# Where the inverse roots of boundary norms are computed, in what order a first weight slab is loaded, and where one value product of the second memory stands

## The chip, the cores and the metric

The kernel runs on one core of a Trainium2 chip. The metric is the device time of one execution in microseconds, the median of several. The engines are named as in the profile: PE is TensorE's matmul, PEld its weight load, DVE is VectorE, ACT is ScalarE, POOL is GpSimd, and SP is SyncE, which here issues DMAs. Each engine works through its own instructions in order; engines wait for one another by semaphores.

## The reference

Two transformer blocks run one after the other on x (512 tokens by 1024), each with its own memory of 256 tokens. Everything is float32. Cut to its skeleton:

```python
def first_block(x, mem, ...):
    mem_n = rmsnorm(mem, mem_norm)
    mk, mv = memory_kv(mem_n, mem_w_kv[0], ...)
    x = mlstm_layer(x, ..., mk, mv, ...)            # A
    k_sh, v_sh = shared_kv(x, ...)                  # reads rmsnorm(x, kv_norm)
    mk, mv = memory_kv(mem_n, mem_w_kv[1], ...)
    return mla_layer(x, ..., k_sh, v_sh, ..., mk, mv, ...)   # B

def second_block(x, mem, ...):
    h = rms_norm(x, g_mix)
    x = x + mixed(h) @ w_out                        # pooling, differential attention, gates
    hc = rms_norm(x, g_cross)
    x = x + memory_cross_attention(hc, rms_norm(mem, g_mem), w_cq, w_ckv, w_co)
    x = x + jnp.square(jax.nn.relu(rms_norm(x, g_mlp) @ w_up)) @ w_down
    return rms_norm(x, g_final)

def rmsnorm(t, g):
    return t * lax.rsqrt(jnp.mean(t * t, axis=-1, keepdims=True) + EPS) * g
```

What matters here is the norm of a token block: the mean square of its 1024 elements, its inverse root, and the scaling of the block. In the cross attention the second memory's values are mem_n times a half of w_ckv, 256 x 1024.

## The kernel before

A float32 product is made of three matmuls (`mm3`): each operand is split into a high and a low half, and high x high, high x low and low x high are summed in PSUM. The high half is made by ACT as a copy (`whi`, `xth`, `mt`, `cvh`), the low half by DVE as a difference (`wlo`, `xtl`, `mt`, `cvl`). Weights come in slabs of 1 MB. SP issues a slab's DMA into one of two raw buffers (`wraw`), and then four pieces of it are split by ACT (L285) and DVE (L286) into one of two pairs `whi`, `wlo`. A raw buffer is loaded again when its four pieces are split. The program is a list of units, `prog`, which `emit` walks in order. A unit issues its matmuls and the work behind them; between units a few pieces of the next slab are split. So the order on each engine is the order of the units with the pieces in between, and it is fixed when the program is built.

x is kept as four token blocks of 128 (tb0 to tb3), each in two halves of 512 (`xs[tb][h]`, in the profile `xall`). The norm of a block has these steps:

- `norm_half`: ACT squares a half and sums it (`junk`, L582).
- `norm_rsqrt`: two instructions on DVE make the mean (`nv`, L586 and L587), one makes a first guess of the inverse root by integer arithmetic (`rsy`, L546). Then `newton` makes six dependent instructions on 128 x 1 elements (L547, L549, and L552 four times, `rsx` and `rst`). They run on POOL unless `eng` is given. In the kernel before it is given for the first memory block alone.
- `norm_scale`: DVE multiplies both halves by `rst` (`xn`, L594 without a gain, L596 with one).
- `norm_T`: PE transposes a half in four blocks (`tr`, L602), ACT and DVE split it (`xth`, `xtl`).

`boundary` orders this between two layers. `op` are the eight products of an output projection, two for each token block; each ends in an addition to `xall` on DVE (L669). For each block come the first product, the transposes of two blocks earlier, the first square, the scaling of the block before, the second product, the second square with `norm_rsqrt`, and then what `mid` gives. The scaling of tb0 stands behind the norm of tb1. Behind the blocks come the first unit of `fa`, the scaling of tb3, the second unit of `fa`, the transposes of tb2, the rest of `fa`, `fb`, and the transposes of tb3. It is used four times: from A to B (no gain, around 455 to 487 us), from B to the second block's mix (846 to 888), ahead of the cross attention (1118 to 1148) and ahead of the feed-forward part (1258 to 1287).

At the start, `load_mem(i)` issues the DMAs of a memory block's two halves, `dma_first(i)` that of the i-th slab. `stat` is the two squares and `norm_rsqrt`; `xst` and `xsc` are the norms and scalings of the four x blocks, which stand between the products of the first memory (`mk0`, in the profile `mkv`).

`cross_v(s)` makes a quarter of the second memory's values: 24 matmuls for each of two memory token blocks into one PSUM bank `cv`, then the split into `cvh` and `cvl`. Its units `cvs` stand at the end of the mix and in the cross boundary.

Of the kernel before, what the change touches and what calls it, by code (L numbers as in the profile page):

```python
# [26 lines left out]
def block_kernel(ctx: ExitStack, tc: tile.TileContext, A: dict, out: bass.AP, stop=None):  # L27
    nc = tc.nc
# [649 lines left out]
    def boundary(op, mid={}, fa=(), fb=(), gain=False):  # L678

        sts = [dict() for _ in range(4)]  # L680
        res = []

        def trans(tb):
            return [U(lambda h=h: norm_T(sts[tb], tb, h, xt_dst(S["xt"])), quiet=True) for h in range(2)]

        def scale(tb):
            return U(lambda: norm_scale(sts[tb], xs[tb], S["gain"] if gain else None), quiet=True)

        for tb in range(4):
            st = sts[tb]  # L690
            res.append(op[2 * tb][0:3] + ("last",))
            if tb > 1:
                res += trans(tb - 2)
            res += [U(lambda st=st, tb=tb: norm_half(st, xs[tb][0], 0), quiet=True)]
            if tb > 1:
                res.append(scale(tb - 1))
            res += [op[2 * tb + 1][0:3] + ("last",),
                    U(lambda st=st, tb=tb: (norm_half(st, xs[tb][1], 1), norm_rsqrt(st)), quiet=True)]
            if tb == 1:
                res.append(scale(tb - 1))  # L700
            res += mid.get(tb, [])
        fa = list(fa)
        return res + fa[0:1] + [scale(3)] + fa[1:2] + trans(2) + fa[2:] + list(fb) + trans(3)
# [227 lines left out]
    def stat(st, srcs, eng=None):  # L931
# [4 lines left out]
    stx = [dict() for _ in range(4)]  # L936
    mT = [[U(lambda i=i, h=h: norm_T(st0[i], i, h, mt_tiles)) for h in range(2)] for i in range(2)]
    xT = [[U(lambda tb=tb, h=h: norm_T(stx[tb], tb, h, xt_dst(S["xt"]))) for h in range(2)] for tb in range(4)]
    xst = [U(lambda tb=tb: stat(stx[tb], xs[tb])) for tb in range(4)]
    xsc = [U(lambda tb=tb: norm_scale(stx[tb], xs[tb], S["gain"])) for tb in range(4)]  # L940
    mk0 = mem_kv_units(0, "mt")
    add(U(lambda: load_mem(1)), U(lambda: dma_first(0)), U(lambda: S.update(gain=gain_tiles(A["a_norm"], eng=nc.sync))), U(lambda: load_x([0])),
        U(lambda: dma_first(1)), U(lambda: load_x([1, 2, 3])), U(load_constants))
    add(U(lambda: stat(st0[0], mem0[0], eng=dve)), U(lambda: norm_scale(st0[0], mem0[0], S["mgain"], inplace=True)),
        U(lambda: stat(st0[1], mem0[1])), mT[0], (None, 1, False, False), mk0[0][0], U(lambda: norm_scale(st0[1], mem0[1], S["mgain"], inplace=True)), mT[1], xst[0],
        (None, 10000, False, False))
    kd = U(lambda: some_constants(5))
    add(mk0[0][1], xsc[0], xst[1], kd, mk0[1], mk0[6], xT[0], xsc[1], xst[2], kd, mk0[2], mk0[7], xT[1], xsc[2], xst[3], kd, mk0[3], xT[2], xsc[3], kd, kd)
# [659 lines left out]
        return U(fn, cslab(("ckv", s), w_ckv, 256 * s, 256))  # L1608

    def cross_v(s):  # L1610
        def fn(w):
            ps = bank([128, 2, 256], "cv")
            for i in range(2):
                m2_product(ps[:, i, :], w, i, True)
            cv = S["cv"]
            c = slice(256 * s, 256 * s + 256)
            return lambda: split(cv[0][:, :, c], cv[1][:, :, c], ps)

        return U(fn, cslab(("ckv", 4 + s), w_ckv, 1024 + 256 * s, 256))

    ckt_ps = {}

# [263 lines left out]

    cvs = [cross_v(s) for s in range(4)]
    oa = outproj("o2a", w_out2, 4, 2, slots=(0,))
    add(rate(2, 2), weave(st[0:1], o2p[0:1]), weave(st[1:2], dp[1][0][1:2] + o2p[1:2]), weave(st[2:3], o2p[2:3] + dp[1][1][1:2]), weave(st[3:4], dp[2][0][0:1]), weave(st[4:5], o2p[3:4] + dp[2][1][0:1]), weave(st[5:6], o2p[4:5] + dp[2][0][1:2]), weave(st[6:7], o2p[5:6] + dp[2][1][1:2]), weave(st[7:8], o2p[6:7] + o2p[7:8] + v2[2:3]), weave(st[8:9], p3[0:1]), weave(st[9:10], v2[3:4] + p3[1:2]), weave(st[10:11], t3[0:1] + t3[1:2]), weave(st[11:12], dg[2:3]), weave(st[12:13], []), weave(st[13:14], dg[3:4] + [U(open_cv)]), weave(st[14:15], oa[0:1]), weave(st[15:16], oa[1:2]), weave(st[16:17], oa[2:3] + oa[3:4]), weave(st[17:18], oa[4:5]), weave(st[18:19], oa[5:6] + oa[6:7]), weave(st[19:20], oa[7:8]), weave(st[20:21], cvs[0:1] + cvs[1:2]), cvs[2:3])
    o2a = outproj("o2b", w_out2, 6, 2, slots=(1,))  # L1890
    if stop == "X":
        add(o2a)
# [69 lines left out]
    add(U(open_cross))  # L1962
    cqi = [cq(h) for h in range(4)]
    h0f, h0r = fm_halves(cqi[0] + cqi[1])
    add(boundary(o2a, fa=cvs[3:4], gain=True), U(open_ca), h0f, h0r)
    fill = [fmu(*u_) for u_ in cqi[2] + cqi[3]]
    st0_, st1_ = csteps([0, 1], {0: 0, 1: 1}), csteps([2, 3], {2: 2, 3: 0})
    add(weave(st0_, fill))
# [265 lines left out]
```

## Time and profile before

| | us |
|---|---|
| median of three runs (1634.8, 1635.64, 1636.66) | 1635.64 |
| the profiled execution | 1637.59 |
| its span | 1635.70 |
| mean granted clock of TensorE in it | 0.983 |

The profile is of one execution. Times in it count from the start of its span; what lies around the span is 1.9 us. PE is busy for 96% of the span, DVE for 65%, ACT for 45% and POOL for 20%. The DMA engines are busy for under 30% in the mean. The chain that ended last is to be read with care here, since an in-order queue that was itself late shows as the work ahead of it. The places at which PE waits, and what stood ahead on the engine that it waited for, are found in the list of waits and the timeline.

### The profile page before, as it was taken

What the parts mean: (1) busy time and instruction counts of PE and PEld (TensorE: products, weight loads), DVE (VectorE), ACT (ScalarE), POOL (GpSimd) and SP (SyncE); (2) the same over time, 40 slices, a digit from 0 to 9 for tenths busy, and PEclk for the clock granted to TensorE, in tenths of its full rate; (3) what the DMA queues carried; (4) which work ended last, traced back from release to release, by engine and by line L of the source; (5) the groups of instructions that cost most, each with busy time, mean ns of one, the idle gap of its engine ahead of it and who ended that gap; (6) DMA issues with size and microseconds to landing.
All of it is one profiled execution on the core that took longest, in us unless ns stands there. A gap on an engine that the chain in (4) does not pass through costs nothing. (4 is left out here: it accounts for less than half of the span.)

```text
span 1635.7 us, 24280 instructions
## 1 busy us (share of the span) xinstructions
PE 1563.6 (96%) x9385; PEld 1359.4 (83%) x9385; DVE 1063.8 (65%) x1980; ACT 743.3 (45%) x1539; POOL 332.6 (20%) x584
## 2 busy tenths in 40 slices
PE   6999999999999999999989999998999999999996
PEld 6889898988788878878869877778987889898986
DVE  6557646565685663667776556567446479686957
ACT  5344434333464543444544334445333463636363
POOL 3100000000030100111211000012000265656663
PEclk9999999999999999999999999999999999999998
DMA  8422223231342221212425331223312224242411
GB/s 268 136 78 62 93 78 88 68 93 65 126 134 67 84 78 53 74 34 67 130 65 172 93 116 54 87 92 125 108 52 77 91 78 142 65 142 61 133 52 52
DMA packets 134795, 152.75 MB, mean 93 GB/s; under 512 B 7616, under 2 KB 120024, under 8 KB 134680
## 3 DMA queue, kind: packets, MB, share of 16 engines
q1 hardware_dynamic: 132376, 144.63, 27.9%
q0 software_dynamic: 2304, 6.57, 1.3%
q8 instruction: 74, 1.21, 0.3%
q14 instruction: 41, 0.34, 0.1%
HBM read 144.88 MB, written 6.31 MB: 92 GB/s over the span
## 5 line engine op out<-in xcount | busy, mean ns | idle before, releaser
L520 PE MATMUL fm<-xth,whi 128*128 128x512 f32 (+1 forms) x824 | 307.7, 373 | 1.0 <-ACT whi L285 0.7
L521 PE MATMUL fm<-xtl,whi 128*128 128x512 f32 (+1 forms) x824 | 306.8, 372 | 1.3 <-DVE xtl L537 1.2
L522 PE MATMUL fm<-xth,wlo 128*128 128x512 f32 (+1 forms) x824 | 306.3, 372 | 0.1
L286 DVE TENSOR_TENSOR wlo<-wraw,whi 128x512 fp32r<-128x512 f32 (+2 forms) x324 | 206.2, 680 | 33.3 <-ACT whi L285 23.8
L285 ACT ACTIVATE whi<-wraw 128x512 fp32r<-128x512 f32 (+2 forms) x324 | 182.6, 619 | 39.5 <-PE op L522 23.1
L521 PEld LDWEIGHTS fm<-xtl,whi 128*128 128x128 f32 x824 | 157.0, 190 | 29.1 <-DVE xtl L537 2.4
L520 PEld LDWEIGHTS fm<-xth,whi 128*128 128x128 f32 x824 | 156.7, 190 | 28.3 <-ACT whi L285 1.0
L522 PEld LDWEIGHTS fm<-xth,wlo 128*128 128x128 f32 x824 | 156.6, 190 | 27.3 <-DVE wlo L286 0.5
L547 POOL TENSOR_TENSOR rsx<-rsy 128x1 f32<-128x1 f32 (+2 forms) x49 | 14.2, 289 | 759.7 <-DVE rsy L546 712.0
L520 PE MATMUL tm<-whi,xth 128*128 128x256 f32 x416 | 116.0, 279 | 0.0
L521 PE MATMUL tm<-wlo,xth 128*128 128x256 f32 x416 | 115.4, 277 | 0.0
L522 PE MATMUL tm<-whi,xtl 128*128 128x256 f32 x416 | 115.4, 277 | 0.0
L669 DVE TENSOR_TENSOR xall<-op,xall 128x512 f32<-128x512 f32 x120 | 81.7, 686 | 47.4 <-PE op L522 47.1
L522 PE MATMUL dn<-whi,ffgl 128*128 128x256 f32 x296 | 83.4, 282 | 0.0
L521 PE MATMUL dn<-wlo,ffgh 128*128 128x256 f32 x296 | 83.3, 282 | 0.0
L520 PE MATMUL dn<-whi,ffgh 128*128 128x256 f32 x296 | 83.3, 281 | 0.0
L521 PEld LDWEIGHTS tm<-wlo,xth 128*128 128x128 f32 x416 | 78.3, 188 | 0.2
L520 PEld LDWEIGHTS tm<-whi,xth 128*128 128x128 f32 x416 | 78.2, 188 | 0.2
L522 PEld LDWEIGHTS tm<-whi,xtl 128*128 128x128 f32 x416 | 78.3, 188 | 0.0
L520 PE MATMUL op<-whi,y0h 128*128 128x512 f32 x160 | 66.8, 418 | 0.0
L521 PE MATMUL op<-wlo,y0h 128*128 128x512 f32 x160 | 63.7, 398 | 0.0
L522 PE MATMUL op<-whi,y0l 128*128 128x512 f32 x160 | 63.7, 398 | 0.0
(588 smaller groups left out, 4062.3 us busy)
## 6 DMA issues: line engine op xcount, KB each, us to landing
wraw<-in_a_w_in_dram SPq DMA_DIRECT2D x23, 1024.0 KB
wraw<-in_w_down_dram SPq DMA_DIRECT2D x19, 512.0 KB
wraw<-in_mem_w_kv_dram SPq DMA_DIRECT2D x8, 1024.0 KB
wraw<-in_b_w_in_dram SPq DMA_DIRECT2D x8, 1024.0 KB
wraw<-in_w_ckv_dram SPq DMA_DIRECT2D x8, 1024.0 KB
wraw<-in_w_in_dram SPq DMA_DIRECT2D x8, 1024.0 KB
wx<-in_w_down_dram SPq DMA_DIRECT2D x13, 512.0 KB
wraw<-in_a_w_out_dram SPq DMA_DIRECT2D x6, 1024.0 KB
```

Of the source, the lines that this page charges most:

```text
L285: act.activation(out=hi[:, s], in_=t[:, s], func=AF.Copy)
L286: dve.tensor_tensor(out=lo[:, s], in0=t[:, s], in1=f(hi)[:, s], op=ALU.subtract)
L520: pe.matmul(out=ps, lhsT=lh, rhs=rh, start=first, stop=False)
L521: pe.matmul(out=ps, lhsT=lh, rhs=rl, start=False, stop=False)
L522: pe.matmul(out=ps, lhsT=ll, rhs=rh, start=False, stop=last)
L547: eng.tensor_tensor(out=x, in0=y, in1=y, op=ALU.mult)
L669: return lambda: dve.tensor_tensor(out=xs[tb][h], in0=ps, in1=xs[tb][h], op=ALU.add)
```

## The change

There are four edits.

1. In `boundary` the Newton steps get `eng=dve`: 16 norms, four at each of the four boundaries.
2. At the start the norms of the second memory block and of the four x blocks get `eng=dve`: 5 norms.
3. At the start the first slab's DMA is issued ahead of the second memory block's two DMAs.
4. `cross_v` becomes two units, one for each memory token block, and the split follows the second. The second of the third quarter (`cvs[2][1:2]`) moves from ahead of the cross boundary into it, behind the products of tb1 (`mid`). The fourth quarter (`fa`) is now two units, so that the scaling of tb3 stands between them.

The counts of instructions on PE, ACT and SP stay the same; 126 instructions move from POOL to DVE.

```diff
@@ -695,7 +695,7 @@
             if tb > 1:
                 res.append(scale(tb - 1))
             res += [op[2 * tb + 1][0:3] + ("last",),
-                    U(lambda st=st, tb=tb: (norm_half(st, xs[tb][1], 1), norm_rsqrt(st)), quiet=True)]
+                    U(lambda st=st, tb=tb: (norm_half(st, xs[tb][1], 1), norm_rsqrt(st, eng=dve)), quiet=True)]
             if tb == 1:
                 res.append(scale(tb - 1))
             res += mid.get(tb, [])
@@ -936,13 +936,13 @@
     stx = [dict() for _ in range(4)]
     mT = [[U(lambda i=i, h=h: norm_T(st0[i], i, h, mt_tiles)) for h in range(2)] for i in range(2)]
     xT = [[U(lambda tb=tb, h=h: norm_T(stx[tb], tb, h, xt_dst(S["xt"]))) for h in range(2)] for tb in range(4)]
-    xst = [U(lambda tb=tb: stat(stx[tb], xs[tb])) for tb in range(4)]
+    xst = [U(lambda tb=tb: stat(stx[tb], xs[tb], eng=dve)) for tb in range(4)]
     xsc = [U(lambda tb=tb: norm_scale(stx[tb], xs[tb], S["gain"])) for tb in range(4)]
     mk0 = mem_kv_units(0, "mt")
-    add(U(lambda: load_mem(1)), U(lambda: dma_first(0)), U(lambda: S.update(gain=gain_tiles(A["a_norm"], eng=nc.sync))), U(lambda: load_x([0])),
+    add(U(lambda: dma_first(0)), U(lambda: load_mem(1)), U(lambda: S.update(gain=gain_tiles(A["a_norm"], eng=nc.sync))), U(lambda: load_x([0])),
         U(lambda: dma_first(1)), U(lambda: load_x([1, 2, 3])), U(load_constants))
     add(U(lambda: stat(st0[0], mem0[0], eng=dve)), U(lambda: norm_scale(st0[0], mem0[0], S["mgain"], inplace=True)),
-        U(lambda: stat(st0[1], mem0[1])), mT[0], (None, 1, False, False), mk0[0][0], U(lambda: norm_scale(st0[1], mem0[1], S["mgain"], inplace=True)), mT[1], xst[0],
+        U(lambda: stat(st0[1], mem0[1], eng=dve)), mT[0], (None, 1, False, False), mk0[0][0], U(lambda: norm_scale(st0[1], mem0[1], S["mgain"], inplace=True)), mT[1], xst[0],
         (None, 10000, False, False))
     kd = U(lambda: some_constants(5))
     add(mk0[0][1], xsc[0], xst[1], kd, mk0[1], mk0[6], xT[0], xsc[1], xst[2], kd, mk0[2], mk0[7], xT[1], xsc[2], xst[3], kd, mk0[3], xT[2], xsc[3], kd, kd)
@@ -1608,15 +1608,18 @@
         return U(fn, cslab(("ckv", s), w_ckv, 256 * s, 256))
 
     def cross_v(s):
-        def fn(w):
-            ps = bank([128, 2, 256], "cv")
-            for i in range(2):
-                m2_product(ps[:, i, :], w, i, True)
+        ps = []
+
+        def fn(w, i):
+            if i == 0:
+                ps.append(bank([128, 2, 256], "cv"))
+            m2_product(ps[0][:, i, :], w, i, True)
             cv = S["cv"]
             c = slice(256 * s, 256 * s + 256)
-            return lambda: split(cv[0][:, :, c], cv[1][:, :, c], ps)
-
-        return U(fn, cslab(("ckv", 4 + s), w_ckv, 1024 + 256 * s, 256))
+            return (lambda: split(cv[0][:, :, c], cv[1][:, :, c], ps[0])) if i else None
+
+        key = cslab(("ckv", 4 + s), w_ckv, 1024 + 256 * s, 256)
+        return [U(lambda w, i=i: fn(w, i), key) for i in range(2)]
 
     ckt_ps = {}
 
@@ -1886,7 +1889,7 @@
 
     cvs = [cross_v(s) for s in range(4)]
     oa = outproj("o2a", w_out2, 4, 2, slots=(0,))
-    add(rate(2, 2), ..., weave(st[20:21], cvs[0:1] + cvs[1:2]), cvs[2:3])
+    add(rate(2, 2), ..., weave(st[20:21], cvs[0] + cvs[1]), cvs[2][0:1])
     o2a = outproj("o2b", w_out2, 6, 2, slots=(1,))
     if stop == "X":
         add(o2a)
@@ -1962,7 +1965,7 @@
     add(U(open_cross))
     cqi = [cq(h) for h in range(4)]
     h0f, h0r = fm_halves(cqi[0] + cqi[1])
-    add(boundary(o2a, fa=cvs[3:4], gain=True), U(open_ca), h0f, h0r)
+    add(boundary(o2a, mid={1: cvs[2][1:2]}, fa=cvs[3], gain=True), U(open_ca), h0f, h0r)
     fill = [fmu(*u_) for u_ in cqi[2] + cqi[3]]
     st0_, st1_ = csteps([0, 1], {0: 0, 1: 1}), csteps([2, 3], {2: 2, 3: 0})
     add(weave(st0_, fill))
```

At the start, DVE's queue from the statistics of the second memory block on. `nv`, `rsy`, `rsx` and `rst` belong to its norm, `mt` is the transposed first memory block, `wlo` the first slab. Before:

```order
L586 TENSOR_SCALAR nv<-nss 128x1
L587 SCALAR_TENSOR_TENSOR nv<-nss,nv 128x1
L546 TENSOR_SCALAR rsy_171<-nv 128x1
L537 TENSOR_TENSOR mt<-tr,mt 128x4x128 x2
L286 TENSOR_TENSOR wlo<-wraw,whi 128x512 x4
L596 SCALAR_TENSOR_TENSOR mem<-mem,rst_173,gain 128x512 x2
```

With the change:

```order
L546 TENSOR_SCALAR rsy_171<-nv 128x1
L547 TENSOR_TENSOR rsx_172<-rsy_171 128x1
L549 TENSOR_SCALAR rsx_172<-rsx_172,nv 128x1
L552 TENSOR_SCALAR rst_173<-rsx_172 128x1
L552 TENSOR_SCALAR rst_173<-rst_173,rsx_172 128x1 x2
L552 TENSOR_SCALAR rst_173<-rst_173,rsy_171 128x1
L537 TENSOR_TENSOR mt<-tr,mt 128x4x128 x2
L286 TENSOR_TENSOR wlo<-wraw,whi 128x512 x4
L596 SCALAR_TENSOR_TENSOR mem<-mem,rst_173,gain 128x512 x2
```

The six Newton steps now stand between `rsy` and the `mt` pair, ahead of the first slab's `wlo`.

At the cross boundary, DVE's queue from the last additions of the mix on; `xall` are the additions of token blocks 0 and 1, `rst_11312` and `rst_11344` their inverse roots. Before:

```order
L537 TENSOR_TENSOR cvl<-cv,cvh 128x2x256
L286 TENSOR_TENSOR wlo<-wraw,whi 128x512 x3
L669 TENSOR_TENSOR xall<-op,xall 128x512
L286 TENSOR_TENSOR wlo<-wraw,whi 128x512
L669 TENSOR_TENSOR xall<-op,xall 128x512
L586 TENSOR_SCALAR nv<-nss 128x1
L587 SCALAR_TENSOR_TENSOR nv<-nss,nv 128x1
L546 TENSOR_SCALAR rsy_11310<-nv 128x1
L669 TENSOR_TENSOR xall<-op,xall 128x512 x2
...
L596 SCALAR_TENSOR_TENSOR xn<-xall,rst_11312,gain 128x512 x2
L669 TENSOR_TENSOR xall<-op,xall 128x512
L537 TENSOR_TENSOR xtl<-tr,xth 128x4x128 x2
```

With the change (`rst_11274` and `rst_11306` are the same two roots):

```order
L669 TENSOR_TENSOR xall<-op,xall 128x512 x2
...
L546 TENSOR_SCALAR rsy_11272<-nv 128x1
L547 TENSOR_TENSOR rsx_11273<-rsy_11272 128x1
...
L669 TENSOR_TENSOR xall<-op,xall 128x512 x2
...
L552 TENSOR_SCALAR rst_11306<-rst_11306,rsy_11304 128x1
L596 SCALAR_TENSOR_TENSOR xn<-xall,rst_11274,gain 128x512 x2
L537 TENSOR_TENSOR cvl<-cv,cvh 128x2x256
L286 TENSOR_TENSOR wlo<-wraw,whi 128x512 x2
L669 TENSOR_TENSOR xall<-op,xall 128x512
L286 TENSOR_TENSOR wlo<-wraw,whi 128x512 x2
L537 TENSOR_TENSOR xtl<-tr,xth 128x4x128 x2
L596 SCALAR_TENSOR_TENSOR xn<-xall,rst_11306,gain 128x512 x2
```

`cvl` and four pieces of `wlo` stand behind the first `xn` now, and ahead of the second; two sets of Newton steps stand ahead of the first.

## Rows read from the trace of the kernel before

**Rows 1.** The page, its first part: busy time in us of each engine, its share of the span, and its instructions.

```profile
PE 1563.6 (96%) x9385; PEld 1359.4 (83%) x9385; DVE 1063.8 (65%) x1980; ACT 743.3 (45%) x1539; POOL 332.6 (20%) x584
```

**Rows 2.** What PE waited for, over the whole span: PE's instruction, the instruction it waited for, us in total, times, longest wait.

```profile
PE tr L602 <- DVE xn L596: 10.9, 5, 3.4
...
PE tr L602 <- DVE mem L596: 9.5, 1, 9.5
...
PE tr L602 <- DVE xn L594: 1.6, 1, 1.6
```

**Rows 3.** The last four of the six Newton steps, line L552, over the whole span: first the steps on POOL that read `rst` and `rsx` (duration in ns: min/median/max; first and last start in us), then, from the list of who waited for the line, one entry (us, times).

```profile
L552 POOL TENSOR_SCALAR rst<-rst,rsx x46: 267/267/1326, 12.9 to 1279.6; 128x1 f32<-128x1 f32 x46
...
  DVE xn L596: 4.0, 5
```

**Rows 4.** The timeline of DVE in the norm of the first memory block: the first and the last of its six steps (start us, duration us).

```profile
5.41 0.16 DVE L547 TENSOR_TENSOR rsx<-rsy 128x1 f32<-128x1 f32 x1
...
6.60 0.21 DVE L552 TENSOR_SCALAR rst<-rst,rsy 128x1 f32<-128x1 f32 x1
```

**Rows 5.** The timeline of the first 16 us, all engines (start us, duration us, engine, line, operation, tiles; in brackets the idle time ahead of it and who ended it). SPq rows are DMA issues on SP's queue.

```profile
3.06 0.91 SPq L109 DMA_DIRECT2D mem<-in_mem_dram  x2
...
4.00 0.43 SPq L197 DMA_DIRECT2D wraw<-in_mem_w_kv_dram  x1
...
9.95 0.63 ACT L582 ACTIVATE junk<-mem 128x512 f32<-128x512 f32 x1 [4.95 <-DMA mem<-in_mem_dram]
...
10.70 0.63 ACT L582 ACTIVATE junk<-mem 128x512 f32<-128x512 f32 x1
...
11.33 1.06 ACT L536 ACTIVATE mt<-tr 128x512 fp32r<-128x512 f32 x2
...
11.65 0.15 DVE L546 TENSOR_SCALAR rsy<-nv 128x1 int32<-128x1 int32 x1
...
11.94 1.29 DVE L537 TENSOR_TENSOR mt<-tr,mt 128x512 fp32r<-128x512 f32 x2
...
13.59 2.19 ACT L285 ACTIVATE whi<-wraw 128x512 fp32r<-128x512 f32 x4 [1.19 <-DMA wraw<-in_mem_w_kv_dram]
...
14.25 2.50 DVE L286 TENSOR_TENSOR wlo<-wraw,whi 128x512 fp32r<-128x512 f32 x4 [1.02 <-ACT whi L285]
...
14.99 0.58 PE L521 MATMUL mkv<-wlo,mt 128*128 128x256 f32 x1
```

**Rows 6.** The timeline of the rest of the start-up, from 20 to 54 us: the second slab's `wlo`, the transposes of the second x block, a `mvl` behind idle time of DVE, and the transposes of the fourth x block.

```profile
23.09 2.50 DVE L286 TENSOR_TENSOR wlo<-wraw,whi 128x512 fp32r<-128x512 f32 x4 [0.17 <-ACT whi L285]
...
38.24 1.51 PE L602 MATMUL tr<-ident,xn 128*128 128x128 f32 x8 [1.75 <-DVE xn L596]
...
47.44 0.69 DVE L537 TENSOR_TENSOR mvl<-mkv,mvh 128x512 fp32r<-128x512 f32 x1 [1.51 <-ACT mvh L536]
...
52.45 1.84 PE L602 MATMUL tr<-ident,xn 128*128 128x128 f32 x8 [1.98 <-DVE xn L596]
```

**Rows 7.** The timeline at the boundary between A and B, 460 to 474 us.

```profile
465.27 0.69 DVE L754 TENSOR_REDUCE ssq<-sq 128x4 f32<-128x512 f32 x1 [1.39 <-ACT sq L752]
...
471.70 1.12 PE L602 MATMUL tr<-ident,xn 128*128 128x128 f32 x8 [1.59 <-DVE xn L594]
```

**Rows 8.** The timeline at the boundary between B and the second block's mix, 848 to 862 us.

```profile
853.11 0.38 PE L521 MATMUL ck<-m2l,whi 128*128 128x256 f32 x1 [0.56 <-DVE m2l L537]
...
859.67 0.69 DVE L537 TENSOR_TENSOR ckl<-ck,ckh 128x512 fp32r<-128x512 f32 x1 [2.12 <-ACT ckh L536]
```

**Rows 9.** The timeline at the boundary ahead of the cross attention, 1116 to 1150 us.

```profile
1117.45 0.73 ACT L539 ACTIVATE y1h<-ym,dcol 128x512 fp32r<-128x512 f32 x1 [1.51 <-DVE ym L1833]
...
1123.24 0.68 DVE L669 TENSOR_TENSOR xall<-op,xall 128x512 f32<-128x512 f32 x1
...
1129.70 1.29 PE L602 MATMUL tr<-ident,xn 128*128 128x128 f32 x8 [2.51 <-DVE xn L596]
...
1132.27 1.41 DVE L596 SCALAR_TENSOR_TENSOR xn<-xall,rst,gain 128x512 f32<-128x512 f32 x2
...
1145.18 1.42 DVE L596 SCALAR_TENSOR_TENSOR xn<-xall,rst,gain 128x512 f32<-128x512 f32 x2 [0.81 <-POOL rst L552]
...
1145.99 1.97 PE L602 MATMUL tr<-ident,xn 128*128 128x128 f32 x8 [3.38 <-DVE xn L596]
```

**Rows 10.** The timeline at the boundary ahead of the feed-forward part, 1260 to 1274 us.

```profile
1263.08 0.69 DVE L669 TENSOR_TENSOR xall<-op,xall 128x512 f32<-128x512 f32 x1 [0.32 <-PE op L522]
...
1264.91 1.41 DVE L596 SCALAR_TENSOR_TENSOR xn<-xall,rst,gain 128x512 f32<-128x512 f32 x2
...
1265.71 1.32 PE L602 MATMUL tr<-ident,xn 128*128 128x128 f32 x8 [1.27 <-DVE xn L596]
...
1272.76 0.39 PE L521 MATMUL fm<-xtl,whi 128*128 128x256 f32 x1 [0.54 <-DVE xtl L537]
```

**Rows 11.** Three windows of 4 us: from:to, length, busy us (and instructions) of PE, PEld, DVE, ACT and POOL, then the granted clock as a share of full speed, the DMA share and GB/s.

```profile
38.00:42.00 4.00, 3.72 (x20) 3.55 (x21) 3.85 (x10) 3.97 (x10) 2.38 (x6) 0.65 0.88 267
470.00:474.00 4.00, 2.41 (x15) 2.04 (x15) 3.18 (x10) 1.54 (x6) 0.58 (x4) 1.00 0.71 202
1145.00:1149.00 4.00, 3.01 (x14) 3.01 (x15) 3.66 (x6) 1.60 (x3) 1.27 (x3) 0.51 0.64 205
```

**Rows 12.** The low halves of the weight pieces on DVE, line L286, over the whole span (duration in ns: min/median/max; first and last start in us; forms).

```profile
L286 DVE TENSOR_TENSOR wlo<-wraw,whi x324: 284/684/707, 14.2 to 1310.9; 128x512 fp32r<-128x512 f32 x158, 128x528 fp32r<-128x528 f32 x2, 128x128 fp32r<-128x128 f32 x2
```

More of the change, by code (lines that the diff above doesn't have):

```diff
@@ L1888, in block_kernel @@
     oa = outproj("o2a", w_out2, 4, 2, slots=(0,))
-    add(rate(2, 2), weave(st[0:1], o2p[0:1]), weave(st[1:2], dp[1][0][1:2] + o2p[1:2]), weave(st[2:3], o2p[2:3] + dp[1][1][1:2]), weave(st[3:4], dp[2][0][0:1]), weave(st[4:5], o2p[3:4] + dp[2][1][0:1]), weave(st[5:6], o2p[4:5] + dp[2][0][1:2]), weave(st[6:7], o2p[5:6] + dp[2][1][1:2]), weave(st[7:8], o2p[6:7] + o2p[7:8] + v2[2:3]), weave(st[8:9], p3[0:1]), weave(st[9:10], v2[3:4] + p3[1:2]), weave(st[10:11], t3[0:1] + t3[1:2]), weave(st[11:12], dg[2:3]), weave(st[12:13], []), weave(st[13:14], dg[3:4] + [U(open_cv)]), weave(st[14:15], oa[0:1]), weave(st[15:16], oa[1:2]), weave(st[16:17], oa[2:3] + oa[3:4]), weave(st[17:18], oa[4:5]), weave(st[18:19], oa[5:6] + oa[6:7]), weave(st[19:20], oa[7:8]), weave(st[20:21], cvs[0:1] + cvs[1:2]), cvs[2:3])
+    add(rate(2, 2), weave(st[0:1], o2p[0:1]), weave(st[1:2], dp[1][0][1:2] + o2p[1:2]), weave(st[2:3], o2p[2:3] + dp[1][1][1:2]), weave(st[3:4], dp[2][0][0:1]), weave(st[4:5], o2p[3:4] + dp[2][1][0:1]), weave(st[5:6], o2p[4:5] + dp[2][0][1:2]), weave(st[6:7], o2p[5:6] + dp[2][1][1:2]), weave(st[7:8], o2p[6:7] + o2p[7:8] + v2[2:3]), weave(st[8:9], p3[0:1]), weave(st[9:10], v2[3:4] + p3[1:2]), weave(st[10:11], t3[0:1] + t3[1:2]), weave(st[11:12], dg[2:3]), weave(st[12:13], []), weave(st[13:14], dg[3:4] + [U(open_cv)]), weave(st[14:15], oa[0:1]), weave(st[15:16], oa[1:2]), weave(st[16:17], oa[2:3] + oa[3:4]), weave(st[17:18], oa[4:5]), weave(st[18:19], oa[5:6] + oa[6:7]), weave(st[19:20], oa[7:8]), weave(st[20:21], cvs[0] + cvs[1]), cvs[2][0:1])
     o2a = outproj("o2b", w_out2, 6, 2, slots=(1,))
```

## The prediction

> **What bounds the kernel now.** I read the busy line of the page first: PE is busy 1563.6 of 1635.7 us [rows 1], so only the 72 us in which it does not run can be changed, and the change touches no matmul's form or count. Then the list of what PE waited for [rows 2]: transposes (`tr`) waited 10.9 us in five waits for a scaled block `xn` with a gain, 1.6 once for one without, and 9.5 at the start for the first memory block. These are the places the change goes to. The wait list names DVE's `xn` as releaser, not what `xn` waited for, so the third view is the line of the Newton steps [rows 3]: DVE's `xn` waited for POOL's `rst` only 4.0 us in five waits. For the rest of those waits DVE was working through its own queue. So at these places DVE's queue is the bound more often than POOL's latency, and what an edit puts into that queue matters more than what it saves on POOL.
>
> **The price of one norm on DVE.** The first memory block's norm already runs on DVE. Its six steps run from 5.41 to 6.81 us, each dependent on the one before: 1.40 us [rows 4]. On POOL one such step takes 0.27 us at the median and up to 1.33 [rows 3], so about 2 to 4 us for six, but nothing else queues there. The change moves 21 norms: 126 instructions and 21 x 1.40 = 29.4 us into DVE. PE pays only where DVE has no idle time ahead of what PE waits for. I go through the five places.
>
> **Start, +6.2.** The first slab's DMA now precedes the second memory block's two. Before, memory was issued at 3.06 and the slab at 4.00; the block's squares started at 9.95 and 10.70, the slab's first `whi` at 13.59 [rows 5]. If transfers are served about in order of issue, the memory is pushed back by at most the slab's own share, 13.59 - 10.70 = 2.9 us. The slab comes sooner, but that buys nothing: on ACT the two squares and the `mt` pair still stand ahead of `whi`. They took from 9.95 to 11.33 + 1.06 = 12.39, so 2.44, and 12.85 + 2.44 = 15.3 is the new start of `whi` (+1.7). On DVE `rsy` goes from 11.65 to 14.55, then come 1.4 of Newton steps, which now stand ahead of the `mt` pair (1.29) and the first `wlo`: about 17.35 against 14.25, +3.1. PE's second matmul waits for that `wlo` (it ran at 14.99), so the first term is +3.1. If the memory is not pushed at all, only the Newton steps count: from the end of `mt` at 13.23 plus 1.4, 14.6, against 14.25: +0.4. I take the upper value because the slab, issued 0.9 after the memory, did land behind it [rows 5].
>
> Then the four norms of x. The first stands ahead of the second slab's `wlo` at 23.09, where DVE was idle 0.17 [rows 6]: +1.2. It delays the release of the raw buffer, and with it the next slab. The second stands between `wlo` pieces ahead of the `xn` that PE waited 1.75 for at 38.24; DVE had several waits of a few tenths for ACT on the way, so I book +0.5 (0 to 1.4). The third meets 1.51 us of idle before 47.44: nothing. The fourth has only dense DVE work ahead of the `xn` for which PE waited 1.98 at 52.45: +1.4 [rows 6]. Sum 3.1 + 1.2 + 0.5 + 1.4 = 6.2, bounds 0.4 + 1.2 + 0 + 1.4 = 3.0 and 7.1.
>
> **First boundary (A to B), +2.3.** Two norms (2.8) are inserted ahead of the second block's `xn`. DVE was idle 1.39 before `ssq` at 465.27, which takes half, and PE already waited 1.59 for that `xn` at 471.70 [rows 7]: +1.4. The last two stand among the pieces of the next slab; I book +0.9, as a third of their 2.8 (bounds 0 and 2.8). Term 1.4 to 4.2.
>
> **Second boundary (B to mix), +1.4.** The first norm stands ahead of four `m2l`, for the first of which PE already waited 0.56 at 853.11: +1.3. The others meet idle DVE, 2.12 us before 859.67 for instance [rows 8]; I book 0.1. Bounds 0 and 2.8.
>
> **Cross boundary, +2.4.** Here two edits meet. With 24 of the `cv` matmuls moved behind the second block pair, the out-projection starts when `y1h` is done, 1117.45 + 0.73, or 1118.2. On DVE `cvl` and four `wlo` pieces (3.0 us; four pieces in a row took 2.50 [rows 5]) leave the stretch ahead of the first two blocks, and two norms (2.8) enter. So `xall` at 1123.24 comes some 3 us earlier, and the first transposes, for which PE waited 2.51 at 1129.70, stay even [rows 9]. But `cvl` and the four pieces now stand between the two `xn`: the second `xn`, at 1132.27, comes at 1132.27 - 3.0 + 2.8 + 3.0 = 1135.1, a new wait of PE of some 2, where it had none. Behind it, two more norms (2.8) and the removal of `cvl` and two pieces (1.9), which go behind the last `xn`, and of the 0.81 in which that `xn` waited for POOL: about +0.1. The last `xn`, at 1145.18, would move by 2.9, and PE, which waited 3.38 for it at 1145.99, with it; I book 2.4, since small idle stretches of DVE lie between [rows 9]. Bounds: 0, if the 24 matmuls fill what PE waits now, and 4.
>
> **FF boundary, +4.1.** The densest place. The first `xn` at 1264.91 now has two norms ahead of it and DVE only 0.32 idle (before 1263.08): 2.8 - 0.3 = +2.5 on the transposes that waited 1.27 at 1265.71. The third norm stands ahead of the `xtl` for which the first ff matmul waited 0.54 at 1272.76: +1.4 more, with 0.2 for the step between. The fourth replaces POOL's, for which the last `xn` waited, off PE's path [rows 10]. Bounds 2.5 and 5.5.
>
> **Clock, +1.0.** After the waits at 38.24 and 1145.99 the granted clock of the next 4 us was 0.65 and 0.51 (0.5 is the 1.2 GHz level, 1.0 the 2.4 GHz one); after the shorter one at 471.70 it was 1.00 [rows 11]. A stretch of 4 us at half clock does 2 us of work. Several waits grow by 1 to 3 us, and new spells are likelier than not at one of them; I book half a spell, bounds 0 and 4.
>
> **Sum.** 6.2 + 2.3 + 1.4 + 2.4 + 4.1 + 1.0 = 17.4. On the profiled execution's 1637.6 that is 1655.0; the median of the runs is 1.95 lower, so **1653.0**. The low ends sum to 3.0 + 1.4 + 0 + 0 + 2.5 + 0 = 6.9, or 1642.5; the high ends to 7.1 + 4.2 + 2.8 + 4 + 5.5 + 4 = 27.6, but they will not all meet.
>
> **Rivals.** (a) *Faster: POOL blocks DVE.* While POOL's steps run beside DVE's, one holds the other up; on POOL a step stretched from 0.27 to 1.33 [rows 3]. If DVE loses as much to each POOL step as the step lasts, 6 x 0.27 = 1.6 us per norm, the move gives back 1.6 and costs 1.4, and the 4.0 us of waiting for `rst` go too: 4.0 + 21 x 0.2 = 8.2 less, against the start's +1.7 for `whi`, so 1629. It decides from a loss of about 1.2 per norm on. Against it: DVE's 324 `wlo` took 684 ns at the median and 707 at most [rows 12], so no `wlo` was ever held for a POOL step. Chance 0.10. The Trainium skill ("SBUF — State Buffer", section "Who interferes with whom") says that DVE with two inputs in SBUF and a reading GpSimd contend for one port pair, and that whoever issues first makes the other block fully; by that rule DVE should lose sometimes. The trace shows POOL losing alone.
>
> (b) *The cover is larger than I think.* DVE is busy 65% of the span [rows 1], and PE's own queue may hide a late `xn`. If only the start's first term (+3.1) and some 2 of the rest remain, 1635.6 + 5 = 1640.7; down to 1636 if the memory isn't pushed either. Chance 0.15, 0.07 of it within 0.2% of now, which is about what a measurement of this kernel can tell from no change (3.3 us).
>
> (c) *More clock spells.* Two or three of the lengthened waits each add a spell at half clock: +4 to 6 over the sum, 1657 to 1660. It counts as part of my forecast.
>
> **How the numbers follow.** The forecast with (c) has 0.75, (a) 0.10, (b) 0.15. Faster 0.10; within 0.2% 0.08, from (b) and the upper edge of (a); slower 0.82. The range leaves out (a), the low part of (b) and sums beyond 1660: 1640 to 1660.
>
> **What would show it.** In the changed kernel's profile: six steps of 1.2 to 1.5 us on DVE behind each `rsy`; the second memory block's first square near 12.9, the first `wlo` near 17.4; PE waits at the five places longer by the terms above, with a new one of about 2 us before the second transposes of the cross boundary. I am wrong if memory still lands near 9.9, if `wlo` or `xn` get shorter once POOL is silent, or if the waits for `xn` fall with the waits for `rst` and nothing takes their place.

## The result, and the profile after

The changed kernel takes 1656.7 us (median of four runs, 1656.5 to 1659.65) against 1635.3 us: a ratio of 1.0134 with a 95% interval of [1.0119, 1.0149]. It is slower by 21.4 us. The profiled execution took 1656.63 us with a span of 1654.9, 19.2 more than that of before.

The page of the changed kernel, its first part. It answers to [rows 1].

```profile
PE 1568.6 (95%) x9385; PEld 1361.0 (82%) x9385; DVE 1088.3 (66%) x2106; ACT 743.1 (45%) x1539; POOL 289.5 (17%) x458
```

DVE has 126 instructions and 24.5 us more; POOL has 126 instructions fewer and is busy for 43.1 us less. PE's busy time grew by 5.0 us with the same 9385 matmuls, so some of them ran slower; the rest of the 19 is waiting. What PE waited for in the changed kernel (as in [rows 2]):

```profile
PE tr L602 <- DVE xn L596: 16.9, 7, 3.9
...
PE mkv L520 <- ACT whi L285: 4.8, 1, 4.8
...
PE tr L602 <- DVE xn L594: 2.9, 1, 2.9
...
PE mkv L521 <- DVE wlo L286: 2.1, 2, 1.5
```

The waits for `xn` grew by 6.0 and 1.3. A wait for `wlo` is new at the start. No engine waits for another's `rst` any more, and the list of who waited for the Newton line L552 is empty. That line (as in [rows 3]), and below it the low halves of the weights, L286 (as in [rows 12]):

```profile
L552 DVE TENSOR_SCALAR rst<-rst,rsx x44: 212/214/216, 6.1 to 1297.1; 128x1 f32<-128x1 f32 x44
```

```profile
L286 DVE TENSOR_TENSOR wlo<-wraw,whi x324: 287/684/709, 17.6 to 1330.0; 128x512 fp32r<-128x512 f32 x158, 128x528 fp32r<-128x528 f32 x2, 128x128 fp32r<-128x128 f32 x2
```

Each of these 44 steps takes 0.21 us on DVE. `wlo` has the same median as before with the 21 norms' steps gone from POOL, so those steps had not been holding it up.

The timeline of the start (as in [rows 5, 6]):

```profile
3.06 0.45 SPq L197 DMA_DIRECT2D wraw<-in_mem_w_kv_dram  x1
...
13.23 0.63 ACT L582 ACTIVATE junk<-mem 128x512 f32<-128x512 f32 x1 [8.28 <-DMA mem<-in_mem_dram]
...
14.61 1.06 ACT L536 ACTIVATE mt<-tr 128x512 fp32r<-128x512 f32 x2
...
14.93 0.15 DVE L546 TENSOR_SCALAR rsy<-nv 128x1 int32<-128x1 int32 x1
...
15.56 2.18 ACT L285 ACTIVATE whi<-wraw 128x512 fp32r<-128x512 f32 x4
...
16.44 1.28 DVE L537 TENSOR_TENSOR mt<-tr,mt 128x512 fp32r<-128x512 f32 x2
...
17.64 2.49 DVE L286 TENSOR_TENSOR wlo<-wraw,whi 128x512 fp32r<-128x512 f32 x4
...
18.37 0.58 PE L521 MATMUL mkv<-wlo,mt 128*128 128x256 f32 x1 [1.55 <-DVE wlo L286]
...
42.67 1.29 PE L602 MATMUL tr<-ident,xn 128*128 128x128 f32 x8 [2.23 <-DVE xn L596]
...
58.15 1.80 PE L602 MATMUL tr<-ident,xn 128*128 128x128 f32 x8 [3.27 <-DVE xn L596]
```

The second memory block lands 3.3 us later (first square 13.23 against 9.95). ACT's `whi` has no bracket: its slab was there, and ACT was busy with the squares and `mt`. DVE's `rsy` is 3.3 late, and the Newton steps put the `mt` pair 1.5 behind it, where it had been 0.3 behind [rows 5]. So `mt` is 4.5 late; `wlo`, ahead of which DVE had been idle for 1.02, starts at 17.64 and is 3.4 late.

DVE's queue behind the third and the fourth x norm. Before:

```profile
39.13 0.15 DVE L546 TENSOR_SCALAR rsy<-nv 128x1 int32<-128x1 int32 x1
39.20 0.68 DVE L763 TENSOR_TENSOR mkn<-mkv,rsx 128x512 f32<-128x512 f32 x1
```

With the change:

```profile
43.56 0.15 DVE L546 TENSOR_SCALAR rsy<-nv 128x1 int32<-128x1 int32 x1
...
45.07 0.68 DVE L763 TENSOR_TENSOR mkn<-mkv,rsx 128x512 f32<-128x512 f32 x1
...
51.65 0.15 DVE L546 TENSOR_SCALAR rsy<-nv 128x1 int32<-128x1 int32 x1
...
53.16 0.68 DVE L537 TENSOR_TENSOR mvl<-mkv,mvh 128x512 fp32r<-128x512 f32 x1
```

The third norm's steps push the work behind them from 4.4 to 5.9 late. The fourth's, behind the `rsy` at 51.65, fill the idle 1.51 that stood ahead of `mvl` at 47.44 [rows 6]: `mvl` is 5.7 late, no more than what stands ahead of the steps.

The timeline at the four boundaries (as in [rows 7 to 10]):

```profile
481.70 1.54 PE L602 MATMUL tr<-ident,xn 128*128 128x128 f32 x8 [2.86 <-DVE xn L594]
...
863.78 0.38 PE L521 MATMUL ck<-m2l,whi 128*128 128x256 f32 x1 [1.78 <-DVE m2l L537]
...
1142.85 1.29 PE L602 MATMUL tr<-ident,xn 128*128 128x128 f32 x8 [1.13 <-DVE xn L596]
...
1148.89 1.32 PE L602 MATMUL tr<-ident,xn 128*128 128x128 f32 x8 [1.95 <-DVE xn L596]
...
1161.54 1.97 PE L602 MATMUL tr<-ident,xn 128*128 128x128 f32 x8 [3.40 <-DVE xn L596]
...
1280.43 0.15 DVE L546 TENSOR_SCALAR rsy<-nv 128x1 int32<-128x1 int32 x1
...
1281.81 0.21 DVE L552 TENSOR_SCALAR rst<-rst,rsy 128x1 f32<-128x1 f32 x1
1281.94 1.41 DVE L596 SCALAR_TENSOR_TENSOR xn<-xall,rst,gain 128x512 f32<-128x512 f32 x2
...
1282.74 1.54 PE L602 MATMUL tr<-ident,xn 128*128 128x128 f32 x6 [3.85 <-DVE xn L596]
...
1291.89 0.39 PE L521 MATMUL fm<-xtl,whi 128*128 128x256 f32 x1 [0.55 <-DVE xtl L537]
```

The wait at 1148.89 is new, at the second transposes of the cross boundary. The rows at 1280 to 1283 show why the waits grew: the second block's steps run from `rsy` to 1282.0, then the first block's `xn`, which needs none of them, and only then PE's transposes, for which PE has waited 3.85 us.

**Where the time went.** I matched PE's instructions of the two traces in order and took the differences of their start times, the lateness of PE. It changes at the start, at the boundaries, and at stretches where one trace has PE at half clock and the other has not; between these it is constant to a few tenths. Windows of 4 us of the changed kernel (as in [rows 11]):

```profile
99.00:103.00 4.00, 3.05 (x14) 3.06 (x15) 3.90 (x11) 1.22 (x4) 0.00 (x0) 0.62 0.14 24
427.00:431.00 4.00, 4.00 (x19) 3.97 (x19) 2.71 (x5) 1.78 (x4) 0.00 (x0) 0.58 0.71 238
482.00:486.00 4.00, 4.00 (x18) 3.39 (x17) 2.96 (x13) 1.69 (x4) 0.00 (x0) 0.57 0.87 303
864.00:868.00 4.00, 4.00 (x22) 4.00 (x22) 2.94 (x11) 1.45 (x4) 0.00 (x0) 0.57 0.00 0
```

The same places of the program in the kernel before, two of the four:

```profile
94.00:98.00 4.00, 3.77 (x31) 3.71 (x32) 3.25 (x9) 1.21 (x4) 0.44 (x3) 1.00 0.26 52
420.00:424.00 4.00, 4.00 (x31) 3.77 (x31) 2.71 (x6) 1.98 (x4) 0.00 (x0) 1.00 0.62 214
```

In the changed kernel's windows the clock was at its lower level (1.2 GHz) for most of the time and at the upper one (2.4 GHz) for the rest; in the two of before it was at the upper one throughout. A spell at the lower level lasts 3.4 us in these traces, now and then 6.8, and one of 3.4 makes PE about 1.7 late where it is busy. The account of the 19.1 us, from the lateness of PE:

| stretch (times of before) | lateness added | of it spells | left | predicted |
|---|---|---|---|---|
| start, to 60 | +5.7 | -1.5 (one at 39 gone) | 7.2 | 6.2 |
| 60 to 454 | +2.8 | +2.8 (at 100 and 428) | 0 | 0 |
| A to B, to 500 | +3.2 | +1.7 (at 482) | 1.5 | 2.3 |
| to 847 | -2.2 | -2.2 (660 gone, 705 shorter) | 0 | 0 |
| B to mix, to 970 | +3.4 | +1.3 (at 864) | 2.1 | 1.4 |
| cross, to 1190 | +1.5 | -1.1 (1145 shorter) | 2.6 | 2.4 |
| feed-forward, to 1290 | +4.7 | +2.1 (at 1281) | 2.6 | 4.1 |
| sum | 19.1 | 3.1 (predicted 1.0) | 16.0 | 16.4 |

The spells are put down by their place in both traces, so the split is good to a few tenths in each line. In the start line, the `mvl` for which DVE was idle before 47.44 waited, through ACT's `mvh`, for products that PE made in the spell at 39; without that spell the kernel before would have been up to 1.5 earlier there, and the change so much later against it.

### The profile page after: what moved, and what is told of

It reads as the page before. It is cut to its first block, busy times and chain, and to the rows that moved or that the text cites. A ratio compares the mean times of both kernels' runs of the same rounds, so it can differ in the third digit from the quotient of the medians.

```text
span 1654.9 us, 24276 instructions
## 1 busy us (share of the span) xinstructions
PE 1568.6 (95%) x9385; PEld 1361.0 (82%) x9385; DVE 1088.3 (66%) x2106; ACT 743.1 (45%) x1539; POOL 289.5 (17%) x458
## 3 DMA queue, kind: packets, MB, share of 16 engines
q8 instruction: 74, 1.21, 0.3%
## 5 line engine op out<-in xcount | busy, mean ns | idle before, releaser
L286 DVE TENSOR_TENSOR wlo<-wraw,whi 128x512 fp32r<-128x512 f32 (+2 forms) x324 | 206.3, 680 | 32.1 <-ACT whi L285 22.5
L547 POOL TENSOR_TENSOR rsx<-rsy 128x4 f32<-128x4 f32 (+2 forms) x28 | 7.8, 279 | 607.5 <-DVE rsy L546 561.3
```

The source lines that it names most:

```text
L286: dve.tensor_tensor(out=lo[:, s], in0=t[:, s], in1=f(hi)[:, s], op=ALU.subtract)
L547: eng.tensor_tensor(out=x, in0=y, in1=y, op=ALU.mult)
```

## The experiments

Ten kernels. All times are medians. The kernel before took between 1635.6 and 1636.4 us on the chips they ran on; each ratio is to the runs of before on the same chip.

**The first edit alone.** Edit to the kernel before:

```diff
-                    U(lambda st=st, tb=tb: (norm_half(st, xs[tb][1], 1), norm_rsqrt(st)), quiet=True)]
+                    U(lambda st=st, tb=tb: (norm_half(st, xs[tb][1], 1), norm_rsqrt(st, eng=dve)), quiet=True)]
```

> The kernel before with the first edit alone: the Newton steps of the 16 boundary norms on DVE. Theory (DVE's queue sets the boundaries, 1.4 us for each norm that meets no idle time): first boundary +1.6 to 2.3, second +1.4 to 2.4, cross +4.8 here (two norms ahead of the first xn and two behind it, no cv work moved away, less 0.81 of waiting for POOL), feed-forward +3.1 to 4.1; sum 11 to 13, with 0 to 3 of half-clock spells 1646 to 1651. Rival (the start makes nearly all of the loss and DVE's idle time covers the boundaries): 1635 to 1638. Rival (POOL's steps had held DVE up): below 1634.

Measured: 1653.4 us, ratio 1.0111 [1.0094, 1.0128]: 17.9 slower. Both rivals are out. It is 2.4 above the theory's upper end, and its mean clock was 0.978 where before had 0.985 (more on that below). Its wait list:

```profile
PE tr L602 <- DVE xn L596: 16.2, 5, 5.4
```

Five waits for `xn`, as before, but 16.2 us where there were 10.9.

**The second edit alone.**

```diff
-    xst = [U(lambda tb=tb: stat(stx[tb], xs[tb])) for tb in range(4)]
+    xst = [U(lambda tb=tb: stat(stx[tb], xs[tb], eng=dve)) for tb in range(4)]
...
-        U(lambda: stat(st0[1], mem0[1])), mT[0], ...
+        U(lambda: stat(st0[1], mem0[1], eng=dve)), mT[0], ...
```

> The kernel before with the second edit alone: the five norms of the start on DVE, the memory still loaded ahead of the slab. Theory: +0.4 (second memory norm), +1.2 (first x block), +0.5 (second), 0 (third), +1.4 (fourth) = 3.5, with clock 1638 to 1641. Rival (the start is bound by DMA landings, so nothing shows): 1634 to 1636.5.

Measured: 1639.9 us, ratio 1.0031 [1.0019, 1.0042], inside the theory's 1638 to 1641. In its trace, as in the changed kernel's, it is the third x norm that made DVE 1.4 later and the fourth that met idle time, where the theory has 0 and 1.4.

**The third edit alone.**

```diff
-    add(U(lambda: load_mem(1)), U(lambda: dma_first(0)), ...
+    add(U(lambda: dma_first(0)), U(lambda: load_mem(1)), ...
```

> The kernel before with the third edit alone: the first slab's DMA ahead of the second memory block's. Theory (ACT's two squares hold the first whi, memory lands some 3 later): first square near 13.2 us, first whi near 15.5, first wlo near 16.2 instead of 14.25; +2 in the start, 1636.5 to 1639. Rival (the earlier slab lets PE start earlier, since the memory norm is needed later): first whi at 12.7 or before, 1633 to 1635.

Measured: 1638.7 us, ratio 1.0014 [1.0002, 1.0026], as the theory had it. Its timeline:

```profile
12.54 0.63 ACT L582 ACTIVATE junk<-mem 128x512 f32<-128x512 f32 x1 [7.53 <-DMA mem<-in_mem_dram]
...
14.88 2.19 ACT L285 ACTIVATE whi<-wraw 128x512 fp32r<-128x512 f32 x4
```

ACT begins `whi` right behind the squares and `mt`, 1.3 later than before, with its slab waiting.

**The fourth edit alone** (`cross_v` in two units, `mid={1: cvs[2][1:2]}`, as in the change).

> The kernel before with the fourth edit alone: the value products in two units, one moved behind the second block pair. Theory (the out-projection starts 1.8 earlier, cvl and four wlo pieces leave the stretch ahead of the first xn and two pieces and cvl go behind the last one, POOL still makes the roots): the wait of 2.51 at the first transposes goes, the one of 3.38 at the last ones falls by 1 to 2; 1633 to 1635. Rival (cvl and the pieces between the first two xn become a new wait of 2 us): 1636 to 1638.

Measured: 1634.6 us, ratio 0.9989 [0.9979, 0.9999]. It is the one edit that gains, 1 to 2 us by itself. PE's waits at the cross boundary in its trace:

```profile
1134.24 1.32 PE L602 MATMUL tr<-ident,xn 128*128 128x128 f32 x8 [1.20 <-DVE xn L596]
...
1146.15 1.93 PE L602 MATMUL tr<-ident,xn 128*128 128x128 f32 x8 [2.65 <-DVE xn L596]
```

The wait of 2.51 at the first transposes is gone, as the theory had it. The last one fell by 0.7, not by 1 to 2, and the wait of 1.20 at the second transposes is new, so the rival's mechanism was there too, at about half its size.

**Room in the queue, without the dependence.** POOL still makes the roots; the same six steps run on DVE behind each `rsy` of the boundaries, and nobody reads them.

```diff
+        if filler:
+            x2, t2 = (tiny(n, f"{n_}{n}") for n_ in ("fsx", "fst"))
+            dve.tensor_tensor(out=x2, in0=y, in1=y, op=ALU.mult)
+            dve.tensor_scalar(out=x2, in0=x2, scalar1=v, scalar2=-0.7468889355659485, op0=ALU.mult, op1=ALU.add)
+            src = x2
+            for c, by in ((-0.87124263, x2), (0.77787455, x2), (-0.77461322, x2), (1.15710291, y)):
+                dve.tensor_scalar(out=t2, in0=src, scalar1=c, scalar2=by, op0=ALU.add, op1=ALU.mult)
+                src = t2
```

> The kernel before, its Newton steps still on POOL, with the same six steps done a second time on DVE behind each rsy of the 16 boundary norms, into tiles that nobody reads. Theory (what the first edit costs is the room in DVE's queue): about as slow as the first edit alone (1653), say 1648 to 1656, since the same 1.4 us stand at the same places; xn may besides wait for POOL. Rival (the cost is that xn now depends on steps of its own engine, or that POOL's absence changes something, not the room): 1635 to 1640.

Measured: 1653.8 us, ratio 1.0104 [1.0091, 1.0117], the same as the first edit alone. At the feed-forward boundary (`fsx` and `fst` are the steps nobody reads):

```profile
1273.40 0.15 DVE L546 TENSOR_SCALAR rsy<-nv 128x1 int32<-128x1 int32 x1
1273.59 0.16 DVE L549 TENSOR_TENSOR fsx<-rsy 128x1 f32<-128x1 f32 x1
...
1274.79 0.21 DVE L553 TENSOR_SCALAR fst<-fst,rsy 128x1 f32<-128x1 f32 x1
1274.92 1.40 DVE L604 SCALAR_TENSOR_TENSOR xn<-xall,rst,gain 128x512 f32<-128x512 f32 x2
...
1275.71 1.97 PE L610 MATMUL tr<-ident,xn 128*128 128x128 f32 x8 [3.87 <-DVE xn L604]
```

PE waits 3.87 where the changed kernel waits 3.85. So the room that six small instructions take in DVE's queue accounts for the cost of the first edit, to within the intervals (2 to 3 us either way). The dependence of `xn` on its own engine and POOL's absence are not needed for it.

**The change without its fourth edit.**

> The changed kernel without its fourth edit (the value products as before). Theory (the fourth edit takes work off DVE ahead of the first xn of the cross boundary, so it makes up there for two of the norms): 2 to 4 slower than the changed kernel, 1658 to 1661, about the sum of the first three edits alone (17.9 + 4.4 + 3.2 = 25.5, or 1661) where they do not overlap. Rival (the fourth edit's cvl and pieces between the first two xn cost as much as they save): 1655 to 1657.

Measured: 1661.4 us, ratio 1.0159 [1.0143, 1.0174], 4.7 above the changed kernel (4.1 by the two ratios) and a little over the expected band. That the fourth edit gains more beside the norms than alone (1 to 2 us) is not shown: the difference is within the intervals, and the mean clock was lower here (0.9765 against 0.980).

**The memory norm behind the first product**, with the third and the fourth edit.

```diff
-        U(lambda: stat(st0[1], mem0[1])), mT[0], (None, 1, False, False), mk0[0][0], U(lambda: norm_scale(...
+        mT[0], (None, 1, False, False), mk0[0][0], U(lambda: stat(st0[1], mem0[1], eng=dve)), U(lambda: norm_scale(...
```

> The kernel before with the fourth edit, the slab first, and the second memory block's norm (on DVE) moved behind the first product of the first memory block, so that its squares no longer stand ahead of the first whi. Theory (in the third edit alone ACT's two squares held whi): first whi near 12.8 us, first mkv near 13.5 instead of 14.27, the second block's transposes a little later; 1633 to 1635, 0 to 1 below the fourth edit alone. Rival (the second memory norm becomes the wait of PE, since it starts after the slab's split): 1636 to 1638.

Measured: 1634.5 us, ratio 0.9994 [0.9985, 1.0003]. Its timeline:

```profile
12.27 2.19 ACT L285 ACTIVATE whi<-wraw 128x512 fp32r<-128x512 f32 x4 [0.37 <-DMA wraw<-in_mem_w_kv_dram]
...
12.95 0.58 PE L520 MATMUL mkv<-whi,mt 128*128 128x256 f32 x1 [1.69 <-ACT whi L285]
```

Now ACT waits for the slab, not the slab for ACT, and PE's first product starts 1.3 earlier than before. So it was the squares ahead of `whi` that made the earlier slab worthless. The kernel's time does not tell it from the fourth edit alone.

**A delay at the start.** Thirty dependent steps on DVE ahead of the first memory scaling in the kernel before.

```diff
+    def delay():
+        t = tiny(1, "fst")
+        src = st0[0]["r"]
+        for _ in range(30):
+            dve.tensor_scalar(out=t, in0=src, scalar1=0.5, scalar2=st0[0]["r"], op0=ALU.add, op1=ALU.mult)
+            src = t
```

> The kernel before with 30 dependent steps on DVE (about 0.25 us each, so 7 us) ahead of the scaling of the first memory block, of which about 2 are covered by the wait for the gain; nothing else changed. It delays all later work by one amount. Theory (half-clock spells of PE fall where waits meet the chip's own beat, so that a shift alone makes some come and others go): the time grows by 5 to 6, with 2 to 3 more or less for spells, 1638 to 1644, and the profile has spells at other places, though each wait is as long as before. Rival (spells come with longer waits only): the same places have spells as before and the time grows by the delay at the first transposes to within 0.5.

Measured: 1636.1 us, ratio 0.9997 [0.9985, 1.001]. Neither came out: no growth can be measured. The delay is there in its trace:

```profile
14.44 1.41 DVE L596 SCALAR_TENSOR_TENSOR mem<-mem,rst,gain 128x512 f32<-128x512 f32 x2
...
18.41 0.58 PE L520 MATMUL mkv<-whi,mt 128*128 128x256 f32 x1 [1.20 <-ACT whi L285]
```

The first product starts 4.1 late (18.41 against 14.27). In that profiled execution PE is only 2.2 late by 45 us, since the spell at 39 is gone, and not late any more by 720, with the spells at 660 gone and at 705 shorter; a spell at 97, which before has not, went the other way. Spells also come and go between executions of one kernel, so one trace does not show that the shift moved them. Something else moved with it, too. The same stretch of the `fm` products, without a wait, before and here:

```profile
1155.00:1171.00 16.00, 16.00 (x136) 16.00 (x135) 4.01 (x7) 3.87 (x7) 0.00 (x0) 1.00 0.00 1
```

```profile
1152.00:1168.00 16.00, 16.00 (x144) 16.00 (x143) 3.97 (x7) 3.88 (x7) 0.00 (x0) 1.00 0.14 48
```

At the same granted clock PE gets through 144 matmuls in 16 us here and 136 before. Over the whole trace, stretches at full clock without waits make PE some 6.8 us earlier than before, more than the delay had cost. So in this execution the delay was made up for by PE's own pace as well as by spells. The median of the runs stays where it was at about the same clock as before (0.984 and 0.985), so there, too, it was not the spells that made up for the delay. What changed the pace is open. This kernel adds a tile; the one with the unread steps adds two, and has such stretches too, slower and faster ones, of up to 1.1 us in 100 us. The others add none, and in their traces the pace differs from before by at most 0.6 us in 100 us, away from the start and from where the order of the work changed.

**PE kept busy in its waits.** The changed kernel with eight transposes of the identity ahead of the real ones at six places.

```diff
+        if h == 0 and tb in warm:
+            for k in range(8):
+                pe.transpose(out=ps[:, k % 4, :], in_=ident, identity=ident)
```

> The changed kernel with eight transposes of the identity (about 1 us at full clock) ahead of the transposes at six of the places where PE waits there: second and fourth x block at the start, second block of the first boundary, second and fourth of the cross boundary, first of the feed-forward boundary. They are written over by the real ones, so no result changes; at these places PE waited 1.9 to 3.9 us and has room for them. Theory (PE's longer waits at these places cost twice, the second time as half clock behind them): the spells behind these places (at 59, 482, 1161 and 1281 us) become fewer, the mean clock rises from 0.980 by 0.002 to 0.004, and 1652 to 1655. Rival (the spells come on the chip's own beat, not with these waits): clock 0.980, 1656 to 1659.

Measured: 1658.1 us, ratio 1.0145 [1.0127, 1.0163], no better than the changed kernel; the mean clock was 0.982 against 0.980. In the windows that answer to 482 and 1281 us:

```profile
481.00:485.00 4.00, 3.50 (x25) 3.21 (x25) 2.96 (x13) 1.70 (x4) 0.22 (x1) 1.00 0.98 316
1283.00:1287.00 4.00, 2.54 (x12) 1.97 (x13) 3.78 (x8) 1.79 (x4) 0.00 (x0) 0.87 0.02 4
```

Behind the first boundary's wait PE is now at full clock, and the feed-forward spell comes later. The clock went as the theory had it and the time did not. The transposes of the identity also left much of the waits as they were: PE still waited 12.6 us for `xn` with a gain, of 16.9. So this does not decide between the two.

**The last block's norm alone on DVE**, on top of the memory norm behind the first product.

```diff
-    add(boundary(o2a, mid={1: cvs[2][1:2]}, fa=cvs[3], gain=True), ...
+    add(boundary(o2a, mid={1: cvs[2][1:2]}, fa=cvs[3], gain=True, on={3: dve}), ...
-    add(U(next_xt_ff), boundary(oc1, fa=uf, gain=True), ...
+    add(U(next_xt_ff), boundary(oc1, fa=uf, gain=True, on={3: dve}), ...
```

> The kernel with the fourth edit, the slab first and the second memory norm moved behind the first product (1634.5), and besides the Newton steps of the last token block alone on DVE at the cross and feed-forward boundaries, the two places where xn of that block waited for POOL (0.81 and 1.63 us before). Theory (only there does POOL's latency end last, and six steps of 1.4 on DVE take less than the steps that POOL still had to do, with little behind them in DVE's queue): 0 to 1.5 less, 1633 to 1634.5. Rival (DVE's queue is what counts there too, since weight pieces stand behind the steps): 1635 to 1637.

Measured: 1633.45 us, ratio 0.9985 [0.9974, 0.9997]: faster than both kernels, by 3.0 and 23. Who waited for L552 in it:

```profile
  DVE xn L596: 1.5, 3
```

It was 4.0 us in five waits [rows 3]. The step from the kernel without these last two norms (the memory norm behind the first product) is 1.1 us, less than the intervals can tell, and so is the step from the fourth edit alone (1634.6, ratio 0.9989). So the gain is that of the edits together: the fourth edit, the reordered start, and three norms on DVE at places where their root ended last or DVE was idle.

## Why the prediction was right

**The queue, not the latency.** The forecast rested on one reading: DVE's `xn` waits for POOL only 4.0 us, so the waits of PE come from DVE's own queue, and work put there is paid. The first edit alone and the unread steps, 1653.4 and 1653.8, show it. Rival (a), that POOL blocks DVE, is out: `wlo` kept its median with the steps gone from POOL, and `xn` did not get faster (746 ns at the median before, 745 after). In the kernel before, 17 `wlo` began while a Newton step ran on POOL; they took 685 ns at the median, the others 684. The Trainium skill's rule on the shared port pair ("SBUF — State Buffer", "Who interferes with whom") would have let DVE lose sometimes; neither [rows 12] nor the same line after shows DVE losing. Rival (b), larger cover, is out with the first edit's 17.9.

**The terms.** The start was predicted with the second memory block's square at 12.85, `whi` at 15.3 and `wlo` at 17.35; it came to 13.23, 15.56 and 17.64, and PE's second matmul was 3.4 late for 3.1. Over the whole start 7.2 for 6.2. Here the forecast had the third and the fourth x norm the wrong way round: the idle 1.51 before 47.44 stands behind the fourth, and the third stands ahead of dense work and cost 1.4. The sum kept its size by luck, since one of the two met that idle stretch either way. The second and third edit alone gave 4.4 and 3.2 by their medians, half-clock spells included. At the cross boundary the three forecasts held: the first transposes even (PE was 12.9 late ahead of them and 13.15 at them), a new wait of 1.95 at the second (some 2), and the last 2.6 later than PE had been (2.4). At the first boundary the first two norms cost 1.5 for 1.4 and the last two nothing that can be seen beside the spell there, for 0.9. At the feed-forward one PE's first transposes were late as forecast (2.6 for 2.5), but the third norm ahead of `xtl` cost PE nothing that can be seen, for 1.6: PE waited 0.55 for that `xtl`, as before [rows 10], because the spell behind the transposes had already made it 2.1 later. The forecast added the two; here they overlap. The second boundary cost 2.1 for 1.4: its first norm gave the forecast 1.2 to 1.3, and the later ones were not all hidden. In sum 16.0 for 16.4; that the start's excess and the feed-forward's shortfall cancel so well is luck.

**The term that was mis-sized** is the clock: +1.0, bounds 0 and 4. The pair of traces shows 3.1. Over the runs it is more. In the 66 runs of the kernel before beside the experiments, the time goes with the mean granted clock (1642.3 us at 0.979, 1632.3 at 0.988): a straight line through them gives 0.93 us for each 0.001. The median clock was 0.985 before and 0.980 after, so 4.7 of the 21.4 us by that line, which leaves 16.7, and 0.007 x 930 = 6.5 of the first edit's 17.9, which leaves 11.4, inside the theory's 11 to 13. The prediction booked half a spell for its lengthened waits; in this pair three came behind such waits (482, 864, 1281). That a wait must grow for a spell to come is not what the traces show, though: those at 100 and 428 us stand behind waits that are as long in both kernels (1.21 before and 1.20 after; 0.76 and 0.76). The second of them, before and with the change:

```profile
418.24 0.51 PE L520 MATMUL st<-qh,kh 128*128 128x512 f32 x1 [0.76 <-ACT kh L536]
```

```profile
425.05 0.50 PE L520 MATMUL st<-qh,kh 128*128 128x512 f32 x1 [0.76 <-ACT kh L536]
```

What decides them is open.

## What to carry to other kernels

Moving small dependent work to an engine can pay only where its latency on the old engine ends last, and it costs wherever the new engine's queue has no idle time ahead of what others wait for: read who waits for the result, and count the microseconds, before moving all of a kind. (The cost is shown here; a gain from the three norms moved in the last experiment could not be told from the noise.) Six instructions on 128 x 1 elements cost 1.4 us of an in-order queue, as much as the scaling of a whole token block. And a transfer that is moved ahead gains nothing while the engine that is to use it has other work in front that waits for the transfer moved back.

## What the runs showed of the hardware

The granted clock of PE drops to half for spells of 3.4 us (now and then 6.8), seven to fourteen times in each traced execution of the kernels here, its last stretch left out, and which waits they follow changes from one execution to another where the waits do not: behind the 0.76 us wait for `kh` the granted clock was 1.00 in one trace (420 to 424 us) and 0.58 in the other (427 to 431). The runs of one and the same kernel spread over 10 us and go with its mean clock. A 128 x 1 step on DVE (`rst<-rst,rsx`) took 0.21 us in 44 of 44 cases, while the same step on POOL ran from 0.27 to 1.33 us, and DVE's `wlo` took no longer when it began beside one (685 ns for 684). And the same matmuls at the same granted clock of 1.00 went through at 136 in 16 us in one kernel and at 144 in another.
